# Parts two and three of each scan step issued one step later, with more buffers

## The chip, the cores and the metric

The kernel runs on one core of a Trainium2 chip. The metric is the device time of one execution in microseconds (us); three runs of the kernel before are shown with their median, and one more execution was recorded by the profiler. A core has five engines with an instruction queue each, worked off in order: TensorE (PE in the profile; its weight loads are PEld), VectorE (DVE), ScalarE (ACT), GpSimd (POOL) and SyncE (SP, which issues most DMAs here).

## The reference, cut to what matters

Two layers of a trunk on 128 context tokens and 512 latent tokens. Layer 0 has, beside a convolution branch, a state-space scan in both directions over chunks of 128 tokens; after it come a gate, a norm, an output projection and a feed-forward part. The change lies in the scan:

```python
def ssd_scan(x, dt, a, bm, cm, h0):
    ...
    xd = (x * dt[..., None]).reshape(b, nc, q, g, r, p)
    la = (dt * a).reshape(b, nc, q, g, r)
    a_cs = jnp.cumsum(la, axis=2)
    seg = a_cs[:, :, :, None] - a_cs[:, :, None, :]
    decay = jnp.exp(jnp.where(causal, seg, -jnp.inf))
    cb = jnp.einsum('bcqgn,bcsgn->bcqsg', cm, bm)
    y_diag = jnp.einsum('bcqsg,bcqsgr,bcsgrp->bcqgrp', cb, decay, xd)
    decay_to_end = jnp.exp(a_cs[:, :, -1:] - a_cs)
    chunk_states = jnp.einsum('bcqgn,bcqgr,bcqgrp->bcgrpn', bm, decay_to_end, xd)
    def step(h, inp):
        s, d = inp
        return h * d[..., None, None] + s, h
    h_last, h_prev = lax.scan(step, h0, (chunk_states, chunk_decay))
    y_off = jnp.einsum('bcqgn,cbgrpn,bcqgr->bcqgrp', cm, h_prev, jnp.exp(a_cs))
    y = (y_diag + y_off).reshape(b, l, nh, p)
```

There are 16 heads in 4 groups, and 5 chunks (one of the context, four of the latent tokens). `y` of both directions and a skip term are summed, gated with `silu(z)` and normed.

## The kernel before

All of the model stays on one core, activations as `[128 channels, tokens]`. A large product is done in three passes over operands that are split into a rounded part and a rest: `weights` loads a tile `raw` (SP), ACT rounds it to `wh` (`split`, L218), POOL takes the rest `wl` (L221), and `mtile_k` issues the matmuls at L229, 48 rows of 320 or 322 columns for an output tile `acc`. A tile is split in two halves; the first third of each row group needs `wh` alone.

The scan is a loop over 20 steps, 5 chunks for each of the 4 groups. A step has three parts, issued in different turns of the loop:

- `scan_a`: the decay. `e` is loaded by `scan_load` (cumulated sums, spread over 128 partitions); ACT or DVE adds the column term (L847, L850, L852), ACT takes exp (L853). `state_step` makes the next state: POOL scales the inputs to `xdd` (L800) and the old state to `hd` (L809), PE multiplies (L802), DVE adds `hn` (L810). PE makes the score matrix (L857), DVE masks it to `cm` (L859), ACT and DVE make the weights `w` of both directions (L866, L869).
- `scan_b`: POOL multiplies `e` by `w` (L875), PE applies it to the values (L879) and the states to the queries (L883); DVE scales the latter into the second `e` (L885), POOL sums both directions to `y` (L887).
- `scan_c`: DVE adds the two (L895; ACT copies `y` for the context chunk, L898), PE turns it (L901), DVE adds it to `yT` (L904).

Between the parts of a turn stand fillers: lists of other work for PE, each filed under a turn. PROJ files the projections of the next group (`short_conv`, L750, L754, L756; transposes L783, copies L785), GATES the eight gate tiles (`gate_after`: 48 matmuls, SiLU on ACT to `gz`, L724, and L734, L740, L741), LNAT and UAT the norm of the convolution branch (L1002, L1006, L1016, L1017, L320) and its split (L1022, L1023). Behind the scan come 8 output tiles (`u_fill`) that cover the norm of `yT`.

The order on the engines isn't the order of the code: a scheduler takes the instructions by their place in the code and by a model of when they are ready, and gives each tile a buffer of its pool when one is free. Tiles with the same tag share `bufs` buffers. PSUM has 4 banks for the small tiles (`misc`) and 2 tiles of two banks for `acc` in this stage. WB is the number of `w` buffers, YB of `y`, XB of `xb`, XDD of `xdd`; the states have the tags `hst0` and `hst1`. `e` has 4 buffers, and the steps with `i % 3 == 2` take theirs from an older tag, `hmt`.

Of the kernel before, what the change touches and what calls it, by code (L numbers as in the profile page):

```python
# [8 lines left out]
F32 = mybir.dt.float32  # L9
# [6 lines left out]
P = 128  # L16
# [9 lines left out]
CK = 31  # L26
WAYS = ("VSS", "SSS", "VSS", "SSS", "VSS")
GRAIN = (2, 2)
WB = 1
XDD = 2  # L30
YB = 3
HD = 1
CM = 2
XB = 7
DTAT = (1, 2)
BANKS = 2
DTAT2 = 4
# [2 lines left out]
MODSP = (3, 3, 2, 0)  # L40
CONV = (0, 0, 0, 0, 2, 2, 2, 1)
CONVP = (3, 2, 2, 2)
GATES = (8, 8, 13, 14, 16, 17, 15, 18)
PROJ = ((0, 1, 2, 3), (4, 5, 6, 7), (9, 10, 11, 12))
LNAT = (0, 2, 3, 11, 12)
UAT = 19
# [90 lines left out]
def _body(nc, tc, st, A, O, dbg):  # L137
# [4 lines left out]
    sm = st.enter_context(tc.tile_pool(name="sm", bufs=2))  # L142
# [6 lines left out]
    def misc():  # L149
        return pools["misc"].tile([P, 512], F32, tag="misc", name="misc") if "misc" in pools else acc()[:, 0:512]  # L150
# [577 lines left out]
    def gate_after(k):  # L728

        t = gz[k] = t640("gz")  # L730
        gate(k, t)
        if k >= 6:
            return
        V.tensor_tensor(yT[:, k, :], yT[:, k, :], t[:, 0:T], op=MULT)  # L734
        if k == 0:
            S.activation(yss, yT[:, k, :], AF.Square)
        else:
            for s in SEGS:
                t = square_tile(s)
                S.activation(t, tok(yT[:, k, :], s), AF.Square)  # L740
                G.tensor_tensor(tok(yss, s), tok(yss, s), t, op=ADD)  # L741
# [17 lines left out]
    def bc4(ap):  # L759
        return ap[:, :, None].broadcast_to([P, ap.shape[1], 64])  # L760

    def heads(ap):
        return ap.rearrange("p (h w) -> p h w", w=64)

    def project(g, r):
# [24 lines left out]
    def col(t, g, c, d):  # L790
        return t[:, c, 8 * g + 4 * d:8 * g + 4 * d + 4]
# [5 lines left out]
    def state_step(r, g, d, c, h, ps=None):  # L797

        xdd = mzp.tile([P, 256], F32, tag="xdd", name="xdd", bufs=XDD)
        G.tensor_tensor(heads(xdd), heads(r["xb"][c][:, 0:256]), bc4(col(dte, g, c, d)), op=MULT)  # L800
        ps = ps or misc()
        PE.matmul(ps[:, 0:256], lhsT=r["xb"][c][:, 256:384], rhs=xdd, start=True, stop=True)  # L802
        hn = mzp.tile([P, 256], F32, tag=f"hst{d}", name="hn", bufs=(3, 4)[d])
        if h is None:
            S.copy(hn, ps[:, 0:256])
            nc.sync.dma_start(O["st"][d][:, 256 * g:256 * g + 256], hn)
        else:
            hd = mzp.tile([P, 256], F32, tag="hd", name="hd", bufs=HD)
            G.tensor_tensor(heads(hd), heads(h), bc4(col(cdec, g, c, d)), op=MULT)  # L809
            V.tensor_tensor(hn, ps[:, 0:256], hd, op=ADD)  # L810
        return hn

    def states(r, g):
        for d in range(2):
            state_step(r, g, d, 0, None)
        h0 = []
        for d in range(2):
            t = mzp.tile([P, 256], F32, tag=f"hst{d}", name="h0", bufs=(3, 4)[d])
            S.dma_start(t, A["h0"][d][:, 256 * g:256 * g + 256])
            h0.append(t)  # L820
        r["hf"], r["hb"] = {1: h0[0]}, {4: h0[1]}
        for c in (4, 3, 2):
            r["hb"][c - 1] = state_step(r, g, 1, c, r["hb"][c])

    def scan_load(i):

        g, c = divmod(i, 5)
        Q[i]["e"] = []
        for d in range(2):
            pool, tag, n = (sm, "hmt", 2) if i % 3 == 2 else (mzp, "e", 4)  # L830
            e = pool.tile([P, 4, P], F32, tag=tag, name="e", bufs=n)
            EQ.dma_start(e, acsd[d:d + 1, 8 * g + 4 * d:8 * g + 4 * d + 4, P * c:P * c + P].broadcast_to([P, 4, P]))
            Q[i]["e"].append(e)

    def scan_a(r, g, c, q):
# [24 lines left out]

        e1 = q["w"] = mzp.tile([P, 4, P], F32, tag="w", name="w", bufs=WB)
        if WAYS[c][2] == "G":
# [8 lines left out]
    def scan_b(r, g, c, q):  # L871

        cs_ = chunk(c)
        e0, e1 = q["e"][0], q["w"]
        G.tensor_tensor(e0, e0, e1, op=MULT)  # L875
        ps = q["ps"] = misc()
        for h in range(4):
            hs = slice(64 * h, 64 * h + 64)
            PE.matmul(ps[:, P + 64 * h:P + 64 * h + 64], lhsT=e0[:, h, :], rhs=r["xb"][c][:, hs], start=True, stop=True)  # L879
        if c:  # L880
            po = misc()
            for d, hp in ((0, r["hf"][c]), (1, r["hb"][c])):
                PE.matmul(po[:, 256 * d:256 * d + 256], lhsT=r["ct"][:, cs_], rhs=hp, start=True, stop=True)  # L883
            t1 = q["e"][1].rearrange("p h w -> p (h w)")
            last = V.tensor_tensor(heads(t1), heads(po[:, 0:512]), bc4(eacs[:, c, 8 * g:8 * g + 8]), op=MULT)  # L885
            q["y"] = mzp.tile([P, 256], F32, tag="y", name="y", bufs=YB)
            G.tensor_tensor(q["y"], t1[:, 0:256], t1[:, 256:512], op=ADD)  # L887

    def scan_c(r, g, c, q):

        cs_ = slice(P * c, P * c + P)
        ps = q["ps"]
        if c:
            y = q["y"]
            V.tensor_tensor(y, ps[:, P:P + 256], y, op=ADD)  # L895
        else:
            y = mzp.tile([P, 256], F32, tag="y", name="y", bufs=YB)
            S.copy(y, ps[:, P:P + 256])  # L898
        for h in range(2):

            PE.transpose(ps[:, 384 * h:384 * h + P], y[:, P * h:P * h + P], ident)  # L901
        for h in range(2):
            k = 2 * g + h
            V.tensor_tensor(yT[:, k, cs_], ps[:, 384 * h:384 * h + P], yT[:, k, cs_], op=ADD)  # L904


    R = [{} for _ in range(4)]
# [39 lines left out]
    mz = tc.tile_pool(name="mz", bufs=1)  # L947
    mzp = mz.__enter__()
    first[3]()
    fillers = [[] for _ in range(22)]  # L950
    for k in range(KD):
        fillers[GATES[k]].append(lambda k=k: gate_after(k))
    for g in range(1, 4):
# [83 lines left out]
    apply = []  # L1037
    Q = [{} for _ in range(20)]
    EQ = nc.sync
    for i in range(-2, 22):  # L1040
        if i + 2 < 20:
            scan_load(i + 2)
        if 0 <= i + 1 < 20:
            g, c = divmod(i + 1, 5)
            if c == 0:
                states(R[g], g)
            scan_a(R[g], g, c, Q[i + 1])
        if 0 <= i < 22:
            for f in fillers[i]:
                f()  # L1050
        if 0 <= i < 20:
            g, c = divmod(i, 5)
            scan_b(R[g], g, c, Q[i])
        if 0 <= i - 1 < 20:
            g, c = divmod(i - 1, 5)
            scan_c(R[g], g, c, Q[i - 1])
            if g == 3 and c in (2, 4):
                apply.append(y_segment(CHUNKED[c == 4]))

# [312 lines left out]
```

## Time and profile before

| what | value |
|---|---|
| median of 3 runs | 1706.73 us (1704.96 to 1707.06) |
| profiled execution | 1706.93 us |
| its span, first to last instruction | 1705.1 us |
| PE busy over the span | 1625.2 us, 95% |
| the scan | about 256 to 510 us of the span |

The profile gives busy time of each engine, groups of instructions by line with what ended the idle time before them, lists of who waited for whom, and a timeline. "Idle before" an instruction is time in which its engine stood still; the arrow behind it names the instruction that released it. A line of the source can stand for many tiles. The granted clock is the share of TensorE's full speed: 1.00 is 2.4 GHz, 0.50 is 1.2 GHz.

### The profile page before, as it was taken

The page shows a single profiled execution, that of the slowest core. Times are in us where ns is not written, and L with a number is a line of the kernel's source. Part 1 is how long each engine was busy: PE and PEld are TensorE (multiplying, and loading weights), DVE is VectorE, ACT ScalarE, POOL GpSimd, SP SyncE. Part 2 cuts the span into 40 slices and gives each one's busy share as a digit, 9 for nine tenths or more (in the row PEclk, how much of TensorE's full clock was granted, in tenths as well). Part 3 has the DMA queues.
Part 4 walks back from the last instruction along what each step waited for, and adds up shares of the span by engine and source line. Part 5 has one row for each costly group of instructions (what it writes and reads, how often), then busy time and mean ns, then how long its engine had stood idle before and what let it go on. Part 6 is the DMA issues. An engine that isn't in the chain of part 4 may idle for free.

```text
span 1705.1 us, 27795 instructions
## 1 busy us (share of the span) xinstructions
PE 1625.2 (95%) x10760; PEld 1564.1 (92%) x10760; DVE 1360.2 (80%) x2406; ACT 692.8 (41%) x1212; POOL 804.5 (47%) x526
## 2 busy tenths in 40 slices
PE   7999998999899989999999999989899999999996
PEld 4898898889799979999999999879799999999996
DVE  7797796978765788899999999875899848718846
ACT  4322236888863254331231232455633323313324
POOL 3142335655653444554465456405356545534544
PEclk9999999999999999999999999999999999999998
DMA  8455433332333443225225422313523222222123
GB/s 307 160 164 189 136 100 87 112 106 71 97 120 119 135 143 88 67 92 187 98 66 160 142 70 81 122 70 93 184 89 94 78 87 70 67 87 75 47 60 117
DMA packets 81911, 189.20 MB, mean 111 GB/s; under 512 B 7540, under 2 KB 33043, under 8 KB 81780
## 3 DMA queue, kind: packets, MB, share of 16 engines
q1 hardware_dynamic: 79268, 184.94, 34.0%
q10 hardware_dynamic: 2512, 2.49, 0.5%
q8 instruction: 85, 1.39, 0.3%
q14 instruction: 46, 0.38, 0.1%
HBM read 183.57 MB, written 3.83 MB: 110 GB/s over the span
## 4 chain that ended last, share of the span: by engine, by line
PE 42%; DVE 24%; issue 2%; ACT 2%; POOL 1%; DMA 0%; DVEq 0%; ACTq 0%; POOLq 0%
PE acc L229 40%; DVE cva L1114 8%; DVE mm L270 6%; DVE x L356 2%; DVE ssq L324 2%; DVE hmt L342 1%; DVE cva L1103 1%; DVE modc L274 1%; PE acc L1233 1%; ACT sqt L320 1%; POOL wl L221 1%; DVE x L1276 1%; PE acc L331 1%; DVE xl L351 0%; DMA mm<-in_w_modT 0%
## 5 line engine op out<-in xcount | busy, mean ns | idle before, releaser
L221 POOL TENSOR_TENSOR wl<-raw,wh 128x512 fp32r<-128x512 f32 (+5 forms) x314 | 561.1, 1795 | 647.9 <-ACT wh L218 645.5
L229 PE MATMUL acc<-xh,wh 128*128 128x320 f32 (+2 forms) x2064 | 488.4, 314 | 11.9 <-ACT wh L218 7.1
L229 PE MATMUL acc<-xh,wl 128*128 128x320 f32 (+2 forms) x2064 | 487.8, 313 | 6.6 <-POOL wl L221 6.6
L1114 DVE SCALAR_TENSOR_TENSOR cva<-acc,cw,cva 128x504 f32<-128x504 f32 (+2 forms) x704 | 479.0, 692 | 16.6
L229 PE MATMUL acc<-xl,wh 128*128 128x320 f32 (+2 forms) x2064 | 489.0, 314 | 1.2 <-DVE xl L351 1.2
L218 ACT CAST wh<-raw 128x512 fp32r<-128x512 f32 (+5 forms) x314 | 237.8, 768 | 563.2 <-PE acc L229 417.0
L229 PEld LDWEIGHTS acc<-xh,wh 128*128 128x128 f32 (+1 forms) x2064 | 351.4, 190 | 17.9 <-ACT wh L218 9.1
L229 PEld LDWEIGHTS acc<-xh,wl 128*128 128x128 f32 (+1 forms) x2064 | 352.1, 190 | 9.5 <-POOL wl L221 8.3
L229 PEld LDWEIGHTS acc<-xl,wh 128*128 128x128 f32 (+1 forms) x2064 | 351.6, 190 | 3.8 <-DVE xl L351 2.0
L229 PE MATMUL acc<-fh,wl 128*128 128x320 f32 (+2 forms) x832 | 206.6, 311 | 2.8 <-POOL wl L221 2.7
L229 PE MATMUL acc<-fh,wh 128*128 128x320 f32 (+2 forms) x832 | 206.9, 311 | 2.2 <-DVE x L356 2.2
L356 DVE SCALAR_TENSOR_TENSOR x<-acc,modc,x 128x128 f32<-128x128 f32 (+2 forms) x240 | 112.4, 498 | 119.7 <-PE acc L229 118.9
L229 PE MATMUL acc<-fl,wh 128*128 128x320 f32 (+2 forms) x704 | 171.9, 311 | 0.0
L229 PEld LDWEIGHTS acc<-fh,wl 128*128 128x128 f32 x832 | 143.6, 188 | 4.5 <-POOL wl L221 4.2
L229 PEld LDWEIGHTS acc<-fh,wh 128*128 128x128 f32 x832 | 143.6, 189 | 2.9 <-issue 2.5
L270 DVE SCALAR_TENSOR_TENSOR mm<-mm 128x1024 f32<-128x1024 f32 x84 | 144.5, 1720 | 2.0 <-DMA mm<-in_w_modT 1.0
L229 PEld LDWEIGHTS acc<-fl,wh 128*128 128x128 f32 x704 | 121.1, 189 | 0.5
L1129 POOL TENSOR_TENSOR cva<-cva 128x640 f32<-128x640 f32 x44 | 72.0, 1637 | 88.2 <-ACT cva L1128 88.2
L270 DVE SCALAR_TENSOR_TENSOR mjunk<-mraw,crow 128x1024 f32<-128x1024 f32 x68 | 96.6, 1420 | 10.7 <-DMA mraw<-in_w_modT 10.3
L1103 DVE SCALAR_TENSOR_TENSOR cva<-acc,cw,cva 128x127 f32<-128x127 f32 x176 | 60.9, 346 | 48.7 <-ACT cva L1099 43.6
L1133 POOL TENSOR_TENSOR fl<-cva,fh 128x640 fp32r<-128x640 f32 x44 | 70.9, 1611 | 34.4 <-ACT fh L1132 34.4
L1128 ACT ACTIVATE cva<-cva 128x640 f32<-128x640 f32 x44 | 32.3, 735 | 120.4 <-DVE cva L1114 120.4
(248 smaller groups left out, 1929.9 us busy)
## 6 DMA issues: line engine op xcount, KB each, us to landing
raw<-in_ffn_w_up SPq DMA_DIRECT2D x88, 512.0 KB, 3.6
mm<-in_w_modT SPq DMA_DIRECT2D x42, 512.0 KB, 3.7
raw<-in_w_in SPq DMA_DIRECT2D x40, 512.0 KB, 3.7
mraw<-in_w_modT SPq DMA_DIRECT2D x34, 512.0 KB, 3.7
e<-acsd SPq DMA_DIRECT2D x40, 256.0 KB, 3.6
raw<-in_ffn_w_down SPq DMA_DIRECT2D x32, 256.0 KB, 2.7
raw<-in_ffn_w_down SPq DMA_DIRECT2D x16, 448.0 KB, 3.5
raw<-in_w_out SPq DMA_DIRECT2D x24, 256.0 KB, 3.4
```

Of the source, the lines that this page charges most:

```text
L218: S.copy(wh[:, ks, :], raw[:, ks, :])
L221: G.tensor_tensor(wl[:, ks, :], raw[:, ks, :], wh[:, ks, :].bitcast(F32), op=SUB)
L229: PE.matmul(part(ps, s), lhsT=wt[:, k, :], rhs=tok(at, s), start=(k == 0 and p == 0), stop=(k == n - 1 and p == 2))
L270: V.scalar_tensor_tensor(junk, in0=raw[:, cs_], scalar=1.0, in1=crow[j][:, cs_], op0=MULT, op1=MULT, accum_out=m[:, 2 * o + j:2 * o + j + 1])
L274: V.tensor_scalar(modc[l][:, i, :], m[:, 0:2], b, None, op0=ADD)
L324: V.tensor_tensor(tok(self.a, s), tok(self.a, s), t, op=ADD)
L356: last = V.scalar_tensor_tensor(tok(x[:, m, :], sub), in0=part(ps, s, o, sub), scalar=gt[:, m, j:j + 1], in1=tok(x[:, m, :], sub), op0=MUL ...
L1103: V.scalar_tensor_tensor(a[:, lo:hi], in0=ps[:, BASE + lo + d:BASE + hi + d], scalar=w(1, c), in1=a[:, lo:hi], op0=MULT, op1=ADD)
L1114: last = V.scalar_tensor_tensor(av[:, r0:r1, c0:c1], in0=pv[:, r0 + dr_:r1 + dr_, c0 + dc:c1 + dc], scalar=w(r, c), in1=av[:, r0:r1, c0:c1 ...
L1128: S.activation(cv[1], cv[1], AF.Silu)
L1129: G.tensor_tensor(cv[0], cv[0], cv[1], op=MULT)
L1133: G.tensor_tensor(l_, cv[0], h_.bitcast(F32), op=SUB)
```

## The change

`scan_b` of a step comes one turn of the loop later than before and `scan_c` with it, so the loop has one turn more. `w` has 3 buffers (1 before), `y` 4 (3), `xb` 8 (7), the states 4 and 5 (3 and 4), and `e` 6 (4); now the steps with `i % 4 == 3` take theirs from `hmt`. Four gate tiles are filed one turn later: the second (8 to 9), the fifth (16 to 17), the sixth (17 to 18) and the eighth (18 to 19). Turn 16 has no gate tile any more.

```diff
-WB = 1
+WB = 3
 XDD = 2
-YB = 3
+YB = 4
 HD = 1
 CM = 2
-XB = 7
+XB = 8
...
-GATES = (8, 8, 13, 14, 16, 17, 15, 18)
+GATES = (8, 9, 13, 14, 17, 18, 15, 19)
...
-        hn = mzp.tile([P, 256], F32, tag=f"hst{d}", name="hn", bufs=(3, 4)[d])
+        hn = mzp.tile([P, 256], F32, tag=f"hst{d}", name="hn", bufs=(4, 5)[d])
...
-            pool, tag, n = (sm, "hmt", 2) if i % 3 == 2 else (mzp, "e", 4)
+            pool, tag, n = (sm, "hmt", 2) if i % 4 == 3 else (mzp, "e", 6)
...
-    fillers = [[] for _ in range(22)]
+    fillers = [[] for _ in range(23)]
...
-    for i in range(-2, 22):
+    for i in range(-2, 23):
         if i + 2 < 20:
             scan_load(i + 2)
...
-        if 0 <= i < 22:
+        if i >= 0:
             for f in fillers[i]:
                 f()
-        if 0 <= i < 20:
-            g, c = divmod(i, 5)
-            scan_b(R[g], g, c, Q[i])
         if 0 <= i - 1 < 20:
             g, c = divmod(i - 1, 5)
-            scan_c(R[g], g, c, Q[i - 1])
+            scan_b(R[g], g, c, Q[i - 1])
+        if 0 <= i - 2 < 20:
+            g, c = divmod(i - 2, 5)
+            scan_c(R[g], g, c, Q[i - 2])
             if g == 3 and c in (2, 4):
                 apply.append(y_segment(CHUNKED[c == 4]))
```

What this does to the engines' queues shows in the fourth group. First ACT, before: from the SiLU `gz` of the gate tile of turn 15 (`acc_4562`) to the rounding of the next tile's weights, `wh_4673`. The number behind a name tells buffers of one name apart.

```order
L724 ACTIVATE gz_4561<-acc_4562 128x128
L724 ACTIVATE gz_4561<-acc_4562 128x512
L1017 ACTIVATE u_645<-u_645,vec_79 128x640 x2
L847 ACTIVATE e_4529<-e_4529,nacs_639 128x128 x4
L866 ACTIVATE w_4660<-cm_4658,dt_637 128x128 x3
L853 ACT_TABLE_LOAD
L853 ACTIVATE e_4527<-e_4527 128x512
L866 ACTIVATE w_4660<-cm_4658,dt_637 128x128
L218 CAST wh_4673<-raw_4671 128x512 x2
```

Now, ACT has such a row of work twice. The first is behind the gate tile of turn 14 (`acc_4423`), up to the weights of the tile of turn 15 (`wh_4548`):

```order
L724 ACTIVATE gz_4422<-acc_4423 128x128
L724 ACTIVATE gz_4422<-acc_4423 128x512
L1017 ACTIVATE u_645<-u_645,vec_79 128x640
L847 ACTIVATE e_4354<-e_4354,nacs_639 128x128
L740 ACTIVATE sqt_4483<-yT_649 128x320
L740 ACTIVATE sqt_4486<-yT_649 128x320
L847 ACTIVATE e_4354<-e_4354,nacs_639 128x128 x3
L847 ACTIVATE e_4356<-e_4356,nacs_639 128x128 x4
L866 ACTIVATE w_4535<-cm_4533,dt_637 128x128 x4
L853 ACT_TABLE_LOAD
L853 ACTIVATE e_4354<-e_4354 128x512
L218 CAST wh_4548<-raw_4546 128x512 x2
```

The second is behind the tile of turn 15 (`acc_4545`), up to the weights of the tile of turn 17 (`wh_4707`):

```order
L724 ACTIVATE gz_4544<-acc_4545 128x128
L724 ACTIVATE gz_4544<-acc_4545 128x512
L866 ACTIVATE w_4649<-cm_4647,dt_637 128x128 x2
L847 ACTIVATE e_4625<-e_4625,nacs_639 128x128 x4
L847 ACTIVATE e_4627<-e_4627,nacs_639 128x128 x4
L866 ACTIVATE w_4694<-cm_4692,dt_637 128x128 x3
L853 ACT_TABLE_LOAD
L853 ACTIVATE e_4625<-e_4625 128x512
L866 ACTIVATE w_4694<-cm_4692,dt_637 128x128
L218 CAST wh_4707<-raw_4705 128x512 x2
```

The rounding of a gate tile's weights stood behind `gz` of the tile in front of it once; now it stands there twice.

PE at the same place, before: between the gate tile of turn 15 and the next one.

```order
L879 MATMUL misc_4626<-xb_4210,e_4257 128x64 x4
L901 MATMUL misc_4511<-con_77,y_4520 128x128 x2
L802 MATMUL misc_4649<-xdd_4650,xb_4222 128x256
L879 MATMUL misc_4737<-xb_4216,e_4371 128x64 x4
L857 MATMUL misc_4649<-cvc_4199,cvb_4069 128x128
L883 MATMUL misc_4742<-h0_4389,cvc_4199 128x256
L883 MATMUL misc_4742<-hn_4413,cvc_4199 128x256
L802 MATMUL misc_4768<-xdd_4769,xb_4228 128x256
L857 MATMUL misc_4768<-cvc_4199,cvb_4069 128x128
L901 MATMUL misc_4737<-con_77,y_4746 128x128 x2
L229 MATMUL acc_4670<-xh_95,wh_4673 128x320
```

Now, on PE, the last rows between the gate tile of turn 14 and that of turn 15 (five more scan rows stand ahead of these: L879, L883 twice, L901, L802):

```order
L879 MATMUL misc_4609<-xb_3480,e_4090 128x64 x4
L883 MATMUL misc_4614<-hn_4108,cvc_3445 128x256
L857 MATMUL misc_4524<-cvc_4181,cvb_4058 128x128
L883 MATMUL misc_4614<-h0_3639,cvc_3445 128x256
L901 MATMUL misc_4494<-con_77,y_4503 128x128 x2
L802 MATMUL misc_4638<-xdd_4639,xb_4204 128x256
L879 MATMUL misc_4659<-xb_4192,e_4240 128x64 x4
L802 MATMUL misc_4683<-xdd_4684,xb_4210 128x256
L857 MATMUL misc_4638<-cvc_4181,cvb_4058 128x128
L901 MATMUL misc_4609<-con_77,y_4618 128x128 x2
L857 MATMUL misc_4683<-cvc_4181,cvb_4058 128x128
L229 MATMUL acc_4545<-xh_95,wh_4548 128x320
```

And on PE between the gate tiles of turns 15 and 17:

```order
L879 MATMUL misc_4771<-xb_4198,e_4354 128x64 x4
L883 MATMUL misc_4776<-h0_4372,cvc_4181 128x256
L883 MATMUL misc_4776<-hn_4396,cvc_4181 128x256
L857 MATMUL misc_4797<-cvc_4181,cvb_4058 128x128
L901 MATMUL misc_4771<-con_77,y_4780 128x128 x2
L879 MATMUL misc_4878<-xb_4204,e_4510 128x64 x4
L883 MATMUL misc_4883<-hn_4528,cvc_4181 128x256
L883 MATMUL misc_4883<-hn_4388,cvc_4181 128x256
L229 MATMUL acc_4704<-xh_95,wh_4707 128x320
```

Scan rows that stood among the matmuls of several gate tiles now stand together at these two places: three L802 and three L857 in the first, four L883 in the second.

## Rows read from the trace of the kernel before

**Rows 1.** The page, part 1: busy us, share of the span, instructions.

```profile
PE 1625.2 (95%) x10760; PEld 1564.1 (92%) x10760; DVE 1360.2 (80%) x2406; ACT 692.8 (41%) x1212; POOL 804.5 (47%) x526
```

**Rows 2.** Windows: busy us of each engine, granted clock, DMA share, GB/s.

```profile
256.00:510.00 254.00, 230.29 (x1472) 215.19 (x1471) 191.57 (x362) 199.93 (x418) 148.83 (x149) 0.97 0.33 97
...
510.00:558.00 48.00, 48.00 (x326) 47.92 (x325) 24.14 (x46) 16.24 (x30) 14.85 (x12) 1.00 0.36 124
```

**Rows 3.** Waits of PE, 255 to 510 us: total us, times, longest.

```profile
PE misc L857 <- DVE hn L810: 6.9, 6, 3.0
PE misc L802 <- POOL xdd L800: 5.3, 6, 1.5
```

**Rows 4.** Timeline of PE: start, us, instruction, idle before and its releaser.

```profile
358.18 0.44 PE L783 MATMUL misc<-con,cvx 128*128 128x128 f32 x2 [1.04 <-DVE yT L904]
...
377.82 1.27 PE L802 MATMUL misc<-xdd,xb 128*128 128x256 f32 x4 [1.00 <-ACT sqt L320]
...
383.01 0.49 PE L857 MATMUL misc<-cvc,cvb 128*128 128x128 f32 x2 [1.55 <-DVE hn L810]
...
401.58 0.49 PE L857 MATMUL misc<-cvc,cvb 128*128 128x128 f32 x2 [0.86 <-DVE hn L810]
...
422.16 0.44 PE L901 MATMUL misc<-con,y 128*128 128x128 f32 x2 [1.21 <-DVE y L895]
...
435.91 0.67 PE L802 MATMUL misc<-xdd,xb 128*128 128x256 f32 x2 [1.70 <-DVE e L885]
```

**Rows 5.** Timeline of PE in the hole.

```profile
458.73 1.10 PE L879 MATMUL misc<-xb,e 128*128 128x64 f32 x8 [0.63 <-POOL e L875]
...
459.95 0.60 PE L883 MATMUL misc<-h,cvc 128*128 128x256 f32 x2
...
460.82 0.59 PE L802 MATMUL misc<-xdd,xb 128*128 128x256 f32 x2
...
462.09 0.49 PE L857 MATMUL misc<-cvc,cvb 128*128 128x128 f32 x2 [0.68 <-DVE hn L810]
...
463.02 0.44 PE L901 MATMUL misc<-con,y 128*128 128x128 f32 x2 [0.44 <-DVE y L895]
...
465.86 0.90 PE L229 MATMUL acc<-xh,wh 128*128 128x320 f32 x2 [2.40 <-ACT wh L218]
...
468.43 0.90 PE L229 MATMUL acc<-xh,wl 128*128 128x320 f32 x2 [1.13 <-POOL wl L221]
```

**Rows 6.** Timeline of ACT in the hole.

```profile
458.26 0.77 ACT L724 ACTIVATE gz<-acc 128x128 f32<-128x128 f32 x2
458.91 1.73 ACT L1017 ACTIVATE u<-u,vec 128x640 f32<-128x640 f32 x2
460.53 1.27 ACT L847 ACTIVATE e<-e,nacs 128x128 f32<-128x128 f32 x4
...
462.69 1.28 ACT L853 ACT_TABLE_LOAD   x1
464.38 0.63 ACT L853 ACTIVATE e<-e 128x512 f32<-128x512 f32 x1 [0.40 <-DVE e L850]
...
465.21 1.12 ACT L218 CAST wh<-raw 128x512 fp32r<-128x512 f32 x2
```

**Rows 7.** Windows behind the hole, columns as in rows 2.

```profile
471.00:472.00 1.00, 1.00 (x5) 1.00 (x5) 0.35 (x1) 1.00 (x3) 0.42 (x1) 0.50 0.68 229
472.00:473.00 1.00, 1.00 (x9) 1.00 (x8) 0.53 (x2) 1.00 (x5) 1.00 (x2) 1.00 0.56 225
```

**Rows 8.** Timeline of POOL in the hole.

```profile
461.79 0.73 POOL L887 TENSOR_TENSOR y<-e 128x256 f32<-128x256 f32 x1 [2.46 <-DVE e L885]
465.87 1.28 POOL L875 TENSOR_TENSOR e<-e,w 128x512 f32<-128x512 f32 x1 [3.36 <-DVE w L869]
467.10 2.50 POOL L221 TENSOR_TENSOR wl<-raw,wh 128x512 fp32r<-128x512 f32 x2
```

**Rows 9.** Waits, 250 to 520 us: total us, times, longest.

```profile
ACT w L866 <- POOL e L875: 2.5, 2, 1.3
```

More of the change, by code (lines that the diff above doesn't have):

```diff
@@ L817, in states @@
         for d in range(2):
-            t = mzp.tile([P, 256], F32, tag=f"hst{d}", name="h0", bufs=(3, 4)[d])
+            t = mzp.tile([P, 256], F32, tag=f"hst{d}", name="h0", bufs=(4, 5)[d])
             S.dma_start(t, A["h0"][d][:, 256 * g:256 * g + 256])
```

## Prediction

> **What bounds the kernel now.** I read the busy shares first: over the whole span TensorE (PE) is busy 95% [rows 1]. So a change pays only where PE stands still or runs at its lower clock. Next, the scan alone, 256 to 510 us: PE is busy 230.29 of 254 us, so 23.7 us of idle time are the most that better order can give back, and the mean granted clock is 0.97; behind the scan, 510 to 558 us, PE has no gap at all [rows 2]. The third view was what PE waits for. The largest entries are L857 behind `hn` of L810 (6.9 us) and L802 behind `xdd` of L800 (5.3 us) [rows 3]: both belong to the state chain and to the head of a step (`state_step`, `scan_a`), which the change leaves where it is. The waits of the moved parts are single gaps in PE's timeline [rows 4], and one stretch that I call the hole [rows 5].
>
> The hole: from 457 us on, behind the gate tile of step 15, PE has only scan work. The next weights are split by ACT, and ACT's queue has `gz` of the tile just finished ahead of them, then `e`, `w`, the exp table, `exp`, and only then the cast `wh` [rows 6]. PE gets going at 465.86 after 2.40 us of waiting, stops again for `wl` (1.13 us), and waits 0.63, 0.68 and 0.44 us on the way: 5.3 us idle [rows 5]. It then runs at a granted clock of 0.50 (1.2 GHz) up to 472, and at 1.00 (2.4 GHz) after that [rows 7]; 4.8 us of matmuls at half speed are another 2.2 us over what they take at full speed. The hole costs 7.5 us (5.3 + 2.2).
>
> **The change part by part.** The same instructions run; what moves is their order on PE, ACT, DVE, POOL and SP. (One thing moves out of the scan: the `e` that sits in the older pool, and is loaded and begun ahead of the scan, is now that of chunk 3 and not of chunk 2. That is four `e` of ACT less in the scan and a few DVE rows more, 1.3 us that no PE wait rests on; nothing.) The three queues that the moved parts pass (POOL with `e*w` L875 and `y` L887, DVE with L885, L895 and L904, SP with the loads of `e`) get one more step of distance between producer and consumer.
>
> *Waits that should go.* L901 behind `y` of L895 at 422.16, 1.21 us; L783 behind `yT` of L904, 1.04 us (a PSUM bank of the third part, now free earlier); L802 behind `e` of L885, 1.70 us; the stops at 377.82 (1.00) and 383.01 (1.55) at the start of the third group; L857 at 401.58, 0.86 us [rows 4]. The last one goes because in the new order 26 rows of L229 stand between L802 and L857 of that step (9 before), 3.8 us of cover at 0.147 us a row, for a chain of 0.6 (POOL `hd`) and 0.42 us (DVE `hn`). Sum 7.4 us.
> *What comes back there.* POOL still has `y`, `wl` and `e*w` between two `xdd` of a group's start (0.73, 1.25 and 1.28 us [rows 8]), and `xdd` has two buffers as before. With those prices I get 0.6 us at the third group and 0.8 us above the waits of today at the fourth. At the first group's end `mu` is now covered by three transposes and not by a whole second part, 0.6 us more. So 7.4 - 2.0 = 5.4 us. The bounds: 0 (every wait replaced by another on the same in-order queues) and 8 us.
>
> *The hole moves and a second one opens.* This is the part that costs. In the new order ACT has, twice, `gz` of a tile ahead of the next tile's `wh`, where the old order has it once and after it three pairs of `wh` in front of the next `gz`.
> Hole one (behind `acc_4423`). ACT: it comes to `gz` 1.8 us late (in the old order the exp table and `w` are in front), then `gz` 0.77, one `u` 0.9, two squares 0.8, eight `e` and four `w` at 0.32 each 3.8, table 1.28, `exp` 0.63, half a `wh` 0.56: 10.5 us [rows 6]. PE's own rows there, with the durations of [rows 5]: 3 x L879 (1.0) + 4 x L883 (0.6) + 3 x L901 (0.44) + 3 x L802 (0.6) + 3 x L857 (0.45) = 9.7 us, threaded on POOL's `hd` and `y` and DVE's `hn`, whose chain ends 12.1 us after the start (last link: `y_4618` behind `hd_4643` behind two sums of squares on POOL). Idle 2.4 us, 0.5 us for `wl`, and the clock between 0 and 2.2 us; I take half, since PE has nearly twice the scan rows that it has in today's hole. Hole one: 4.0 us.
> Hole two (behind `acc_4545`, 48 rows or 7.1 us later). ACT: `gz` 0.77, eight `e` and six `w` 4.5, table 1.28, `exp` 0.63, half a `wh` 0.56: 7.7 us. PE's rows: 2 x L879, 4 x L883, L857, L901: 5.3 us. Then four L229, then L879 of the fourth chunk, which waits for POOL's `e*w` (1.28), which waits for DVE's last `w`, which stands behind L885, which waits for the L883 just issued; and `wl` (1.25) is behind that `e*w` on POOL. From the end of the tile to steady matmuls 11.9 us, 6.3 of them busy: 5.6 us idle, and 2.2 us of clock as in today's hole. Hole two: 7.8 us. Bounds: 2.5 us (only ACT's sum less PE's rows, clock kept) to 9 us.
> Together 11.8 for 7.5 us: 4.3 us lost. Two table loads more (48 for 46 in the whole order, 1.28 us each) stand inside these sums or beside PE work.
>
> What the new buffers do by themselves is little: ACT's wait for the single `w` buffer is 2.5 us in 2 places [rows 9], beside 95% of PE.
>
> Sum: -5.4 + 4.3 = -1.1 us on the profiled execution's 1706.93 us (its span of 1705.1 and 1.8 around it), which lies 0.2 us above the median of 1706.73: **1705.8 us**, no change.
>
> One rule speaks against the change. ACT's exp starts 0.40 us behind the table load of 462.69, and that gap is a wait for DVE [rows 6]. The Trainium skill, "ScalarE: Activation LUTs", section "What ACT_TABLE_LOAD costs", adds a drain of about 1.38 us to each load of 1.283 us; by that estimate, with one or two loads on the path of each hole, the sum would come to some 1709 us. The trace shows the load's length and no drain, so the sum goes without.
>
> **The rivals.** *Faster.* PE's clock stays at 2.4 GHz in both holes and the links on DVE and POOL fall between, so that hole one costs 2.9 and hole two 3.9 us, 0.7 less than today's; the other waits go with almost no return (-6.6): 1706.9 - 7.3 = **1699.6**. For it: a scan with one more step of slack has all `e*w` and `y` ready early. Against: the waits that it does not touch (L857, L802) are 12 of the 23.7 us.
> *Slower.* The place is ACT's queue at the fourth group: twice `gz`, `e`, `w`, table and `exp` stand in front of the `wh` that PE needs next. If PE falls to 1.2 GHz in both (7.5 us for hole one, 8.6 for hole two, 8.6 us more than now) and the group starts give back half (-3.0): 1706.9 + 5.6 = **1712.5**. It decides from the point where the holes cost 6 us more than today's. For it: the present hole did just this [rows 5, 7]. Against: hole one is filled with twice the PE work.
> *It does nothing.* The state chain orders PE in any case, and each wait of the moved parts is replaced by the chain's, one row later: **1707**.
>
> **How the numbers follow.** Forecast 0.42 (its own range 1703 to 1709), faster 0.28, slower 0.26, nothing 0.04. A measurement of this kernel can tell about 0.2% (3.4 us) from no change, so 1703.3 to 1710.1 counts as the same: 0.46; faster 0.28; slower 0.26. With these the range of 8 in 10 reaches to 1699 and to 1712.5.
>
> **What would show it.** Right: PE's idle time from the scan's start to its end is 20 to 24 us; L901, L879 and L885 are nearly gone from the list of what PE waits for; L857 and L802 remain with 9 to 12 us; two stretches with a wait on `wh` or `wl` of over 1 us each stand some 20 us apart near 455 to 485, with a granted clock of 0.5 in at least one. Wrong: only one such stretch, or none (then 1700); a third one, or a wait on `e*w` at L879 of several us before that (then over 1710); any change behind 560 us.

## The result

The changed kernel takes **1718.2 us** (1715.16 to 1723.12) against 1706.7 us before: slower by 0.78%, with a 95% interval of 0.67 to 0.90%. The forecast was 1705.8 us, in a range of 1699 to 1712.5; the time lies 5.7 us above its upper end and on the other side of the kernel before.

The recorded execution of the changed kernel took 1723.1 us (a span of 1721.3 us, 16.2 us more than before). It is the slowest of its runs, and so is that of a second recording (e16 below, 1723.2 us); the median of 1718.2 us is some 5 us below both. So the trace shows about 5 us more loss than the medians do.

### The profile after

The page's first part, columns as in [rows 1]:

```profile
PE 1636.9 (95%) x10760; PEld 1573.1 (91%) x10760; DVE 1354.5 (79%) x2406; ACT 695.1 (40%) x1214; POOL 805.8 (47%) x526
```

PE is busy 11.7 us longer with the same 10760 instructions; the granted clock of the windows shows where rows took longer. The two windows that answer to [rows 2]:

```profile
256.00:510.00 254.00, 228.23 (x1410) 213.45 (x1409) 173.07 (x342) 192.11 (x400) 144.14 (x144) 0.93 0.29 90
510.00:558.00 48.00, 46.06 (x300) 44.06 (x299) 38.64 (x70) 25.77 (x47) 18.52 (x15) 1.00 0.42 146
```

In the scan the mean granted clock is 0.93 (0.97 before), and in 254 us PE gets through 1410 instructions (1472 before), though it is idle for only 2 us more.

To place the loss I cut the recorded execution at ACT's first copy to `xb` of each group (L785) and at the first matmul on `yh`. Idle is the length of a stretch less PE's busy time. Clock is half of the busy time spent at a granted 0.50, from windows of 1 us: what those rows would have saved at 1.00. Both in us:

| stretch of the span before / after | before: idle + clock | after | second recording of after |
|---|---|---|---|
| up to the scan, 0 to 259 / 262 | 17.8 + 5.1 | 19.4 + 7.6 | 19.2 + 7.7 |
| first group, to 309 / 314 | 6.1 + 3.3 | 11.2 + 0.0 | 10.9 + 0.0 |
| second group, to 357 / 362 | 2.3 + 0.0 | 2.1 + 3.0 | 3.2 + 5.0 |
| third group, to 421 / 426 | 4.5 + 0.0 | 2.4 + 1.7 | 2.4 + 0.0 |
| fourth group, its first 35 us | 4.4 + 0.0 | 3.0 + 3.1 | 3.0 + 2.9 |
| the rest, to `yh` at 560 / 577 | 7.6 + 2.5 | 10.2 + 7.3 | 10.0 + 7.4 |

Length less idle less clock, from the first `xb` copy to `yh`, is 270.7 us before and 270.5 after, and 269.7 to 273.4 in all kernels below without added work; behind `yh` all take 1144 to 1145 us. So idle time and the lower clock are the whole account: in the scan +4.0 us idle and +9.4 us clock. **More than two thirds of the scan's loss is clock.**

What PE waits for from 255 to 580 us, the first seven entries: total us, times and longest, answering to [rows 3]:

```profile
PE misc L802 <- POOL xdd L800: 7.7, 6, 1.9
PE misc L857 <- DVE hn L810: 4.7, 3, 3.0
PE misc L901 <- DVE y L895: 4.1, 2, 2.3
PE misc L783 <- ACT xb L785: 3.6, 1, 3.6
PE misc L879 <- POOL e L875: 2.5, 2, 1.4
PE misc L883 <- DVE yT L904: 1.9, 1, 1.9
PE misc L783 <- ACT cvx L756: 1.4, 1, 1.4
```

Five of the six single waits of [rows 4] are gone; the sixth (377.82) has grown. Elsewhere longer ones are new. Here are three (the second is the one that grew), in PE's timeline (start, us, instruction, idle before and its releaser):

```profile
314.56 0.69 PE L783 MATMUL misc<-con,cvx 128*128 128x128 f32 x2 [3.57 <-ACT xb L785]
...
377.28 1.27 PE L802 MATMUL misc<-xdd,xb 128*128 128x256 f32 x4 [1.92 <-POOL xdd L800]
...
444.09 1.22 PE L802 MATMUL misc<-xdd,xb 128*128 128x256 f32 x2 [1.85 <-POOL xdd L800]
```

The first is the largest new wait, and the clock is at 0.50 behind it (columns as in [rows 7]):

```profile
315.00:316.00 1.00, 1.00 (x7) 1.00 (x6) 1.00 (x3) 0.73 (x2) 1.00 (x2) 0.50 0.00 0
```

The transposes L783 need PSUM banks that ACT's `xb` copies free. ACT in that stretch:

```profile
308.26 0.69 ACT L847 ACTIVATE e<-e,nacs 128x128 f32<-128x128 f32 x2 [4.61 <-DMA e<-acsd]
308.97 1.28 ACT L853 ACT_TABLE_LOAD   x1
310.27 0.63 ACT L853 ACTIVATE e<-e 128x512 f32<-128x512 f32 x1
310.81 1.26 ACT L866 ACTIVATE w<-cm,dt 128x128 f32<-128x128 f32 x4
...
314.05 1.20 ACT L785 COPY xb<-misc 128x384 f32<-128x384 f32 x3
```

ACT stands 4.61 us on a load of `e`, with the copies queued behind it. SP issued that load when POOL was done with the `y` that reads the old `e` in the buffer (303.19 + 0.73 us), and that `y` stood behind `wl`, `e*w` and `wl`. POOL, and then SP's queue:

```profile
298.15 2.50 POOL L221 TENSOR_TENSOR wl<-raw,wh 128x512 fp32r<-128x512 f32 x2 [5.48 <-ACT wh L218]
300.60 1.32 POOL L875 TENSOR_TENSOR e<-e,w 128x512 f32<-128x512 f32 x1
301.89 1.34 POOL L221 TENSOR_TENSOR wl<-raw,wh 128x512 fp32r<-128x512 f32 x1
303.19 0.73 POOL L887 TENSOR_TENSOR y<-e 128x256 f32<-128x256 f32 x1
```

```profile
299.45 4.15 SPq L205 DMA_DIRECT2D raw<-in_w_in  x2
303.95 0.57 SPq L832 DMA_DIRECT2D e<-acsd  x1
```

SP's queue is worked off in order, and the second `raw` load in front of this `e` had waited for the second `wl` (301.89 + 1.34 us): SP came to the `e` at 303.65 us, so its buffer held it for 0.3 us only. The same stands in the second recording. Of ACT's waits for loads of `e`, before and after (255 to 530 us: total us, times, longest)

```profile
ACT e L847 <- DMA e<-acsd: 4.2, 4, 1.9
ACT e L847 <- DMA e<-acsd: 11.6, 6, 4.6
```

three (4.61, 0.58 and 2.66 us, 7.9 of the 11.6) are for loads that SP issued within 0.8 us of a `raw` load which had waited for `wl`. SP's waits at `raw` rose from 90.2 us to 115.1:

```profile
SPq L205 <- POOL wl L221: 90.2, 23, 11.7
SPq L205 <- POOL wl L221: 115.1, 20, 20.3
```

Those at loads of `e`, for a buffer, fell from 139 to 111 us.

The second hole is there as forecast, 13.7 us behind the first. PE's timeline in it:

```profile
463.09 0.44 PE L901 MATMUL misc<-con,y 128*128 128x128 f32 x2 [2.25 <-DVE y L895]
...
476.74 0.44 PE L901 MATMUL misc<-con,y 128*128 128x128 f32 x2 [1.86 <-DVE y L895]
478.35 1.97 PE L879 MATMUL misc<-xb,e 128*128 128x64 f32 x8 [1.17 <-POOL e L875]
...
484.57 1.11 PE L879 MATMUL misc<-xb,e 128*128 128x64 f32 x4 [1.38 <-POOL e L875]
485.84 0.90 PE L229 MATMUL acc<-xh,wl 128*128 128x320 f32 x2 [0.16 <-POOL wl L221]
```

and the windows behind it, columns as in [rows 7], the granted clock third from the right:

```profile
477.00:478.00 1.00, 0.18 (x2) 0.00 (x0) 0.95 (x4) 0.98 (x3) 0.98 (x1) 0.80 0.00 0
478.00:479.00 1.00, 0.66 (x3) 0.66 (x4) 1.00 (x2) 0.91 (x2) 0.29 (x1) 0.50 0.00 0
...
490.00:491.00 1.00, 1.00 (x5) 1.00 (x5) 0.03 (x1) 1.00 (x3) 0.90 (x1) 0.50 0.11 41
491.00:492.00 1.00, 1.00 (x8) 1.00 (x7) 0.00 (x0) 0.71 (x2) 1.00 (x2) 0.87 0.00 0
```

Hole two has 1.86 + 1.17 + 1.38 + 0.16 = 4.6 us idle, and 13.7 us at 1.2 GHz, of which PE is busy 11.4: half of that, 5.7 us, is lost.

### The profile page after: what moved, and what is told of

Read it like the earlier page. It is cut to its first block, busy times and chain, and to the rows that moved or that the text cites. A ratio compares the mean times of both kernels' runs of the same rounds, so it can differ in the third digit from the quotient of the medians.

```text
span 1721.3 us, 27786 instructions
## 1 busy us (share of the span) xinstructions
PE 1636.9 (95%) x10760; PEld 1573.1 (91%) x10760; DVE 1354.5 (79%) x2406; ACT 695.1 (40%) x1214; POOL 805.8 (47%) x526
## 3 DMA queue, kind: packets, MB, share of 16 engines
q10 hardware_dynamic: 2512, 2.49, 0.5%
## 4 chain that ended last, share of the span: by engine, by line
PE 57%; DVE 29%; ACT 5%; issue 4%; POOL 3%; DMA 2%; ACTq 0%; DVEq 0%; POOLq 0%; SPq 0%
PE acc L229 50%; DVE cva L1114 8%; DVE mm L270 6%; DVE x L356 2%; DVE mjunk L270 2%; DVE ssq L324 2%; DVE hmt L342 1%; DVE modc L274 1%; DVE cva L1103 1%; POOL wl L221 1%; PE misc L695 1%; DMA e<-acsd 1%; PE acc L1233 1%; ACT sqt L320 1%; DMA mraw<-in_w_modT 1%
## 5 line engine op out<-in xcount | busy, mean ns | idle before, releaser
L229 PE MATMUL acc<-xh,wh 128*128 128x320 f32 (+2 forms) x2064 | 491.3, 316 | 9.1 <-ACT wh L218 4.7
L270 DVE SCALAR_TENSOR_TENSOR mjunk<-mraw,crow 128x1024 f32<-128x1024 f32 x68 | 96.3, 1417 | 12.0 <-DMA mraw<-in_w_modT 11.6
```

What stands on the lines that cost most here:

```text
L229: PE.matmul(part(ps, s), lhsT=wt[:, k, :], rhs=tok(at, s), start=(k == 0 and p == 0), stop=(k == n - 1 and p == 2))
L270: V.scalar_tensor_tensor(junk, in0=raw[:, cs_], scalar=1.0, in1=crow[j][:, cs_], op0=MULT, op1=MULT, accum_out=m[:, 2 * o + j:2 * o + j + 1])
```

## The experiments

Theories on the table: **H**, the `e` begun ahead of the scan is now that of step 3, in ACT's queue ahead of `cx`; **G**, the places of the gate tiles (no tile in step 16); **D**, the delay of parts two and three by itself; **E**, the delayed second part holds `e` longer, loads of `e` come late, and ACT's queue stands. All in one table (ratio to the kernel before in the same session, 95% interval; ACT's waits for loads of `e` in the scan, idle and clock from first `xb` copy to `yh`, in us of the recorded execution). The recorded execution is one run and need not be near the median: e7's (1712.2 us) and e15's (1705.5 us) are the fastest of theirs.

| kernel | median | ratio | waits for `e` | idle + clock |
|---|---|---|---|---|
| before | 1706.7 | 1 | 4.2 | 25.0 + 5.7 |
| changed | 1718.2 | 1.0067 to 1.0090 | 11.6 | 29.0 + 15.1 |
| e16, changed again | 1719.95 | 1.0071 to 1.0099 | 11.1 | 29.5 + 15.3 |
| e1, changed, `e` of every third step in the older pool | 1723.4 | 1.0090 to 1.0118 | 15.3 | 35.5 + 10.7 |
| e2, before, `e` of every fourth step there, 6 `e` | 1705.5 | 0.9992 to 1.0010 | 4.7 | 21.1 + 6.5 |
| e3, changed, old gate places | 1714.4 | 1.0041 to 1.0066 | 12.4 | 25.8 + 11.0 |
| e4, before, all new buffers | 1704.5 | 0.9983 to 1.0001 | 2.9 | 21.4 + 7.7 |
| e5, third part alone delayed | 1711.9 | 1.0021 to 1.0043 | 4.9 | 24.4 + 8.1 |
| e6, second part alone delayed | 1713.9 | 1.0025 to 1.0052 | 11.2 | 26.8 + 11.8 |
| e7, changed, gate tiles 6, 7 in steps 16, 15 | 1716.3 | 1.0044 to 1.0072 | 11.8 | 24.5 + 12.6 |
| e8, changed, 3 `xdd` | 1718.9 | 1.0059 to 1.0083 | 11.0 | 29.8 + 13.9 |
| e9, before, new gate places | 1708.9 | 1.0004 to 1.0021 | 2.1 | 26.3 + 5.9 |
| e10, e6 with old gate places | 1718.9 | 1.0060 to 1.0086 | 12.1 | 30.9 + 4.6 |
| e11, changed, 8 `e`, 2 `w` | 1711.3 | 1.0012 to 1.0041 | 7.6 | 26.1 + 7.4 |
| e12, changed, spare matmuls | 1717.3 | 1.0046 to 1.0071 | 11.3 | 24.7 + 9.7 |
| e13, before, `e` of every fourth step in the older pool, 4 `e` | 1712.1 | 1.0022 to 1.0049 | 11.1 | 26.2 + 7.4 |
| e14, e10 with 8 `e`, 2 `w` | 1713.3 | 1.0036 to 1.0062 | 10.6 | 28.5 + 5.3 |
| e15, e11 with e7's gate places | 1709.4 | 1.0010 to 1.0027 | 8.2 | 22.2 + 6.7 |
| e17, before, 8 `e`, 2 `w` | **1702.25** | 0.9956 to 0.9980 | 1.3 | 22.0 + 6.7 |
| e18, before, spare matmuls | 1704.0 | 0.9971 to 0.9990 | 5.0 | 22.6 + 3.3 |

### What the parts of the change cost: e1 to e6, e9

e1 (changed kernel) and e2 (kernel before) turn the rule of the older pool round:

```diff
-            pool, tag, n = (sm, "hmt", 2) if i % 4 == 3 else (mzp, "e", 6)
+            pool, tag, n = (sm, "hmt", 2) if i % 3 == 2 else (mzp, "e", 6)   # e1; e2 the other way, in before
```

> The changed kernel (1718.2 us) with the older pool's e given back to every third step, as in the kernel before, so that the e begun ahead of the scan is again that of step 2; the pool of e keeps 6. Theory H (the eight rows of L847 of step 3 stand in ACT's queue ahead of cx of L681 before the scan, PE waits 3.86 us there for 1.63 and its clock falls): the scan's first xb copies come at 259 and not at 262 us, and 3 to 4.5 us come back: 1714 to 1715. Rival D (all of the loss is in the scan's own delay): 1717 to 1719.

> The kernel before (1706.7 us) with one part of the change alone: the older pool's e for every fourth step and six buffers of e. No step is delayed. Theory H: PE's wait at L685 near 155 us grows from 1.6 to about 3.9 us, the scan starts 3 to 4.5 us later, and the kernel takes 1709.5 to 1711. Rival D: 1706 to 1708.

H falls as the cause. e2 has the longer wait before the scan:

```profile
155.15 1.89 PE L685 MATMUL misc<-cx,dfl 128*128 128x512 f32 x2 [3.57 <-ACT cx L681]
```

and yet no loss in time. In all kernels with step 3's `e` there, idle time up to the scan is 18.8 to 21.4 us, in those with step 2's 17.8 to 18.8: one or two us, not four. (What the clock costs up to the scan differs where nothing else does: the instructions there are the same in the changed kernel, 7.6 us, in e7, 1.5, and in e8, 3.4. That part of the first table says nothing of the change.) e1 took away its own test: with every third step in the older pool and the second part a step later, the load for a step waits for a buffer that is freed only in the same turn. ACT waits 15.3 us for `e`, and the kernel is 5 us slower still. That result first pointed to E.

e3 puts the gate tiles back; the gate is then taken before the last chunk's third part has added its sum, so it is a timing only. e9 gives the kernel before the new places:

```diff
-GATES = (8, 9, 13, 14, 17, 18, 15, 19)
+GATES = (8, 8, 13, 14, 16, 17, 15, 18)   # e3
+GATES = (8, 9, 13, 14, 17, 18, 15, 18)   # e9, in before
```

> The changed kernel (1718.2 us) with the gate tiles where they were (8, 8, 13, 14, 16, 17, 15, 18). Theory G (the second hole near 476 us, 10.6 us of idle and half-clock time, comes from the places of the gate tiles): the second hole closes and 5 to 8 us come back: 1710 to 1713. Rival D (the delay of the second and third part opens it, wherever the tiles stand): 1716 to 1720.

> The kernel before (1706 us) with the gate tiles placed as in the change (8, 9, 13, 14, 17, 18, 15; the last one in step 18, as the third part asks) and no part delayed, no buffers added. Theory G (a step without a tile, 16, opens a second hole by itself): 1709 to 1713, with two stretches of half clock between 450 and 500 us. Rival D (the hole needs the delay): 1705 to 1708.

e3 gives back 4 us, e9 loses 2 (0.04 to 0.21%); both lie between what G and D expected. By these two, G is a share of the loss and not all of it; e10 below takes even that back.

e4 is the kernel before with every new buffer:

> The kernel before (1706.7 us) with all the buffers of the change (3 of w, 4 of y, 8 of xb, 4 and 5 of the states, 6 of e) and no delay; e of every third step stays in the older pool and the gate tiles where they are. Theories H, G and D: 1705 to 1708, since no wait for a buffer holds PE. Rival B (more buffers alone let the scheduler put e and w ahead of the weight casts in ACT's queue): 1710 or more.

No loss, as all theories but B had it. e5 and e6 delay one part alone (e6 with the last gate tile in step 18):

```diff
-        if 0 <= i - 1 < 20:
-            scan_b(R[g], g, c, Q[i - 1])
+        if 0 <= i < 20:
+            scan_b(R[g], g, c, Q[i])        # e5; e6 leaves this and has scan_c at Q[i - 1]
```

> The changed kernel (1718.2 us) with only the third part (scan_c) one step later; scan_b stands where it stood before; buffers, pools and gate tiles as changed. Theory P (parts): e*w, L879 and L883 of the second part are what gathers PE's waits into single long ones, so this kernel loses little: 1705 to 1710, with less than 18 us at half clock in the scan (before 13.6, changed 34.1). Rival Q (the third part does it, with its transposes L901 in front of the casts): 1714 to 1719.

> The changed kernel with only the second part (scan_b) one step later, scan_c directly behind it in the same step as two steps' distance is not kept; the last gate tile in step 18 and not 19, as the third part asks. Theory P: the loss is here: 1713 to 1719, with more than 24 us at half clock in the scan. Rival Q: 1705 to 1710.

The third part alone costs 5.7 us, the second 7.7, both 12. e6 came as P expected, and so did the time at half clock (27.3 us in e6, 17.1 in e5), but e5's 1711.9 us lies outside P and Q: neither part is the loss alone. They differ in kind, though: only with the second part delayed do ACT's waits for `e` rise (11.2 against 4.9).

### Single waits and single holes: e7, e8, e10, e12

```diff
-GATES = (8, 9, 13, 14, 17, 18, 15, 19)
+GATES = (8, 9, 13, 14, 17, 18, 16, 15)   # e7
```

> The changed kernel with the two free gate tiles (6 and 7) in steps 16 and 15 and not in 15 and 19, so that no step from 13 to 18 is without one. The instructions up to hole two stand as in the changed kernel. Theory G (the empty step 16 opens hole two, 4.6 us of idle and 5.9 us of clock): hole two closes or shrinks to under 4 us: 1709 to 1713. Rival (ACT's queue there has gz, e, w and exp ahead of wh whatever tile comes): hole two stays, 1716 to 1720.

Hole two shrinks to its first wait (1.86 us at L901) and 3 us of half clock, but a wait of 2.49 us comes up at L962, near the scan's end, and only 2 us are left over. The trace went as G, the time as the rival.

> The changed kernel with three buffers of xdd for two; the order of all engines is nearly the same. PE waits 7.7 us in six places for xdd at L802, and the clock falls behind two of them (near 378 and 443 us, 2.2 and 3.4 us lost). Theory X (those waits are for the buffer): 3 to 8 us come back, 1710 to 1715. Rival Y (POOL's queue of y, wl and e*w holds xdd, not the buffer): 1717 to 1720.

Rival Y. With three `xdd` the waits move on along the state chain: at the scan's start L802's second wait goes, and L857's grows from 3.0 to this:

```profile
275.36 0.80 PE L857 MATMUL misc<-cvc,cvb 128*128 128x128 f32 x2 [5.12 <-DVE hn L810]
```

e10 is e6 with `GATES = (8, 8, 13, 14, 16, 17, 15, 18)`:

> The changed kernel with only the second part one step later and the gate tiles where the kernel before has them; e of every fourth step in the older pool and the buffers as changed. Beside e6_b_only (1713.9 us) it differs in the places of the gate tiles alone. Theory G: 1707 to 1710, the last stretch of the scan (from 455 us on) loses 10 us or less in idle and half-clock time. Rival D: 1712 to 1715, 14 us or more lost there.

Above both: 1718.9 us. The old places, better by 4 us in e3, are worse by 5 here. Order itself moves this kernel by some 5 us in either direction, so a change of one place proves little of that place.

e12 puts 24 matmuls on ready operands into hole two (`fillers[16]`); their result is not used:

> The changed kernel (1718.2 us) with 24 more matmuls of 128 x 320 on operands that lie ready, at hole two (between the rows of L879 that follow the tile before it); they write a bank that nobody reads, so the result is as before, and cost 24 x 0.147 = 3.5 us at full clock. Theory C (PE's clock falls because PE stands still, and hole two costs 4.6 us of idle and 5.9 us of clock): the idle time takes them up and the clock stays up: 1712 to 1715, no stretch of half clock near 477 to 492 us. Rival S (they stand ahead of L883, and the chain behind it moves by as much): 1720 to 1722.

```profile
470.65 0.75 PE L1043 MATMUL acc<-xh 128*128 128x320 f32 x4
...
473.30 2.03 PE L1043 MATMUL acc<-xh 128*128 128x320 f32 x12
...
477.30 1.08 PE L879 MATMUL misc<-xb,e 128*128 128x64 f32 x8 [0.65 <-DVE e L885]
...
479.68 0.56 PE L229 MATMUL acc<-xh,wl 128*128 128x320 f32 x2 [0.67 <-POOL wl L221]
```

```profile
478.00:479.00 1.00, 1.00 (x8) 0.75 (x7) 1.00 (x2) 1.00 (x3) 1.00 (x2) 1.00 0.06 16
...
490.00:491.00 1.00, 1.00 (x9) 1.00 (x8) 1.00 (x1) 0.17 (x1) 1.00 (x2) 1.00 0.67 164
```

The waits of hole two fall from 4.6 to 1.3 us, though PE has 3.5 us more to do, and the clock stays at 1.00. The last stretch loses 6.5 + 1.6 us instead of 10.2 + 7.3; less the 3.5 us of spare work, 6 us are gained in the trace (5.4 to 5.7 in the scan's length against the two recordings). In the medians only 1 to 3 us of that are seen, in the ratios 3 to 5 (the two recordings are the slowest of their runs), and 1717.3 us lies in the range of neither C nor S. Theory C holds for the mechanism; its size in the time stays uncertain.

### The loads of `e`: e11, e13, e14, e15, e17

```diff
-            pool, tag, n = (sm, "hmt", 2) if i % 4 == 3 else (mzp, "e", 6)
+            pool, tag, n = (sm, "hmt", 2) if i % 4 == 3 else (mzp, "e", 8)   # e11, with WB = 2
```

> The changed kernel (1718.2 us) with eight buffers of e for six and two of w for three. Theory E (ACT stands 4.61 us at L847 for an e whose load waited on SP for POOL's y to free its buffer; the xb copies stand behind it, and PE waits 3.57 us at L783 and loses 3.0 us of clock): ACT's waits for loads of e fall from 11.6 to under 5 us, PE's wait at L783 near 314 us goes, and 4 to 6 us come back: 1712 to 1714. Rival (the loads come as late, by SP's queue or by w): 1717 us or more.

7 us come back, more than the 4 to 6 expected, though ACT's waits did not fall under 5 us. PE's wait at L783 falls from 3.57 to 0.89 us and that clock fall is gone; ACT's waits, total us, times, longest:

```profile
ACT e L847 <- DMA e<-acsd: 7.6, 5, 2.8
```

But of the 10.6 us of idle time and clock that the scan saves in the recording, 9.1 lie in the last stretch (6.7 + 1.7 us for 10.2 + 7.3), and the changed kernel's ACT has no wait for a load of `e` behind 400 us. So for the larger part of the gain no path from `e` to PE is shown, and another order of the queues, SP's among them, could explain it as well. e11 also takes a `w` buffer away.

E must also work the other way: e13 leaves every part where it was, and takes a step's room from `e` (`i % 4 == 3` with 4 buffers; e2 with 6 lost nothing).

> The kernel before (1706 us) with no part delayed, and only the rule of the older pool changed (e of every fourth step there), with four buffers of e as before: a step's e then has one step less of room, as the second part's delay takes it away in the change. e2_before_hoist3, with six, took 1705.5 us. Theory E (loads of e that wait for a buffer hold ACT's queue, and with it PE): ACT's waits for loads of e rise from 4.2 to over 9 us, 1710 to 1714. Rival (e11 was only another order of ACT's queue): 1705 to 1708.

```profile
ACT e L847 <- DMA e<-acsd: 11.1, 7, 3.0
```

As E said: 6.1 us lost with no delay at all, and the waits are in sum those of the changed kernel. e2, with two buffers of `e` more and otherwise the same, took 1705.5 us with 4.7 us of them. This pair is the cleanest evidence for E; yet of the 6.0 us that the scan loses more than in e2, 5.4 lie in the last stretch, and there again no path from a load of `e` is shown. e14 is e10 with the room of e11, e15 joins e11 and e7:

> e10_b_only_oldgates (1718.9 us: second part one step later, gate tiles at the old places) with eight buffers of e for six and two of w for three. Theory E: ACT's waits for loads of e fall from 12.1 to under 8 us and 5 to 8 us come back: 1711 to 1714. Rival: 1717 to 1720.

> e11_e8_w2 (1711.3 us: the change with eight buffers of e and two of w) with the two free gate tiles in steps 16 and 15, as in e7_gates_16, which gave 2 us. If the two causes add up: 1708 to 1710. If the places of the tiles only shuffle the order: 1710 to 1714.

Both times came as expected (5.6 us back, and 1709.4). In e14, though, the waits only fell from 12.1 to 10.6 us, so that not all of its gain is E's. e17 gives the kernel before the same room:

```diff
-WB = 1
+WB = 2
-            pool, tag, n = (sm, "hmt", 2) if i % 3 == 2 else (mzp, "e", 4)
+            pool, tag, n = (sm, "hmt", 2) if i % 3 == 2 else (mzp, "e", 8)
```

> The kernel before (1706 us), no part delayed, with eight buffers of e for four and two of w for one. Theory E: ACT's waits for loads of e are 4.2 us in the kernel before, of which little stands in front of what PE needs: 1703.5 to 1706, same within what can be measured. If the room for e had been short there already: under 1703.

```profile
ACT e L847 <- DMA e<-acsd: 1.3, 2, 0.7
```

**1702.25 us, 0.20 to 0.44% faster than before**, and faster than either kernel, under the range of E and as expected if the room for `e` had been short there already. e17 gives `w` a second buffer too, and that was not tried alone; e4, with three `w` and six `e`, gained at most 0.17%.

### Spare work in the old hole, and the changed kernel again: e18, e16

e18 puts the 24 matmuls into the hole of [rows 5], behind the third part of turn 15:

> The kernel before (1706 us) with 24 more matmuls of 128 x 320 on operands that lie ready, between the scan's rows at the hole of 457 to 468 us (5.3 us of idle, 2.2 us of clock); they cost 24 x 0.147 = 3.5 us at full clock and their result is not used. Theory C (idle time takes them up, the clock stays up): idle and half-clock time behind 456 us fall from 10.1 to 5 to 6 us, and the time is 1704 to 1706. Rival S (the chain behind them moves by as much): 1708 to 1710.

```profile
456.00 0.83 PE L1043 MATMUL acc<-xh 128*128 128x320 f32 x4
...
457.93 2.62 PE L1043 MATMUL acc<-xh 128*128 128x320 f32 x16
...
468.00 0.56 PE L229 MATMUL acc<-xh,wl 128*128 128x320 f32 x2 [1.13 <-POOL wl L221]
```

Of the waits in the hole (5.3 us) 1.13 remain, and from 456 us to `yh` no row runs at 0.50. Work without use, 3.5 us of it, makes the kernel 0.10 to 0.29% faster.

> The changed kernel, unaltered, for a second profile and for a time beside the others of this call: 1717 to 1719.5. The waits of PE should stand at the same places (L783 near 314, L802 near 377 and 444, the two holes near 463 and 477 us) with the same lengths within 0.3 us; the clock may fall behind some of them only.

Eighteen of the twenty waits of PE in the scan that both recordings list repeat within 0.02 us. L783's is 3.17 us for 3.57, and L857's at 349 us 1.84 for 0.60. The clock falls again behind L783, near 444 us and in both holes; the fall near 378 is missing, and one behind the longer wait, at 351, is new.

## Why the prediction was wrong, point by point

- **The waits that should go went**, but for the one at the third group's start: 6.4 of the 7.4 us of [rows 4].
- **What comes back there was mis-sized: 2.0 us forecast, some 8 measured.** The third group's start has 1.92 and 0.46 us (0.6 forecast), the fourth's 0.82 and 1.85, 1.2 more than before (0.8 forecast); the first group 1.06 us at L857 (290 us) and 1.41 and 0.26 at its end, the second 0.60; and the second group's start, for which the sum had no term, 3.57 and 0.80 us. Idle time from the first `xb` copy to the last stretch is 18.7 us for 17.3: no gain, and 1.4 us under the lower bound of 0 that I gave it.
- **The step that failed there** is "The three queues that the moved parts pass ... get one more step of distance". I counted SP's loads of `e` among what gains distance. Measured, ACT's waits for them rose from 4.2 to 11.6 us, and in front of the `xb` copies one of them cost 3.57 us of PE and then 3.0 us of clock. I had looked at ACT's order only in the fourth group, and nowhere at SP's, where `raw` loads that wait for POOL's `wl` stand in front of the `e`.
- **The two holes: right in place and chain, wrong in the clock.** L901 behind `y`, L879 behind `e*w` behind `w` behind L885, and then `wl` is the chain I wrote down. Idle of hole two 4.6 us (5.6 forecast), of hole one 2.9 (2.9). But no wait for `wh` appears in either, though each sum had opened with ACT's queue ahead of `wh`; and 2.2 us of clock were taken for hole two, from the hole of before, and it was 5.7 (1.6 in hole one, 1.1 forecast). The last stretch lost 7.4 us more than before, not 4.3. (The 2.2 us were read low: half of 4.8 is 2.4, and the trace gives 2.5. PE's rows of hole one add up to 9.9 us and not 9.7. Neither moves the forecast by more than 0.3 us.)
- **The clock at the group starts had no term.** 7.8 us are lost to it before the last stretch (3.3 before, all in the opening). I priced each single wait by its idle time alone; behind the longer ones (3.57 us at 314, 1.92 at 377, 0.82 + 1.85 at 444) the clock stood at 0.50 for 3.4 to 6.8 us.
- **The buffers and the moved `e` cost nothing**: right for time (e4, e2); the `e` ahead of the scan has some 1.5 us of idle time, for which I had nothing.
- **The rivals.** "Slower", 1712.5 us, named ACT's queue at the fourth group, and 7.4 us of the scan's 13.4 are lost there; but PE waits there for `y` and `e*w`, not for ACT's `wh`, and it too left the group starts with half of the gain. What I called the bound of the holes (9 us for hole two) was passed (10.3).
- **The signs named.** Two stretches near 455 to 485 us came, 13.7 us apart and not 20, and the waits for `wl` in them are 0.23 and 0.16 us, not over 1; PE's idle time in the scan is 25.8 us and not 20 to 24; L857 and L802 have 12.4 us and more (9 to 12 named); L901 and L879 did not leave the list, since they head the holes. What was named for a time over 1710 us (a third stretch, a long wait at L879 ahead of them) did not come, and the time did.
- **The rule weighed there.** ACT's exp at 310.27 us starts 0.01 us behind the table load of 308.97 (1.28 us). The drain of about 1.38 us that the Trainium skill, "ScalarE: Activation LUTs", section "What ACT_TABLE_LOAD costs", adds to a load does not show here either, and the sum was right to leave it out; the 1709 us by that estimate would have been too low as well.

What stays open: with the same number of buffers for `e` and the better gate places, the delayed kernel (e15, 1709.4) is still 7 us behind the undelayed one (e17, 1702.25). Their recorded executions show 3.4 us of it, 2.9 before the scan. And why eight buffers for four living steps (6 and the older 2) serve worse than six for three is not settled. E is supported by times in both directions, but its effects (5 to 7 us) are hardly larger than the 5 us that a change of order alone brings; one of its waits is followed to PE, and that load stood in SP's queue behind `raw` rather than waiting for its buffer. No run moved the `raw` loads out of that queue.

## What to carry to other kernels

Starting a consumer later holds its inputs longer: count the buffers of every tile on the way, loads included, and ask whose in-order queue will stand on a load that comes late, what is queued behind it, and what stands in front of the load in the queue that issues it. Where TensorE is the bound, price a wait by its idle time plus the half speed after it, and distrust a change that turns many short waits into few long ones, even if their sum falls. When an order comes from a scheduler, test a cause in both directions (give it, take it away): a single placement moved this kernel by 5 us either way.

## What the runs showed of the hardware

In the scan of the changed kernel, in two recordings, the granted clock fell to 0.50 at single gaps of PE of 1.84 to 3.57 us and at a pair of 0.82 and 1.85, and stayed there for 3.4 to 13.7 us, while PE was mostly busy again (11.4 of 13.7 us from 477.6 to 491.3). Behind other gaps it did not fall: the 3.04 us at L857 in the scan's opening cost the kernel before 3.3 us of clock and the changed one nothing. It does not do so alike in each execution: of one and the same program two recordings shared four falls in the scan and each had one that the other lacked, and in stretches with the same instructions the loss was 1.5 to 7.7 us. With 24 matmuls on ready operands in the hole, 3.5 us at full speed, it stood at 1.00 through it, in both kernels.
